# Weights laid out by the host, and no transposes in the fold of the cross-attention weights

## The chip, the cores and the metric

The kernel runs on one core of one Trainium2 chip. The metric is the device time of one execution in microseconds (us). The kernel before was run three times: 2549.39, 2549.66 and 2551.5 us, so its median is 2549.66 us. Lower is better.

## What is computed

The reference is one layer of an encoder in float32, on 2048 tokens of width 1024, with 256 memory tokens:

```
u = rms_norm(h, g_mix_pre);  z = u @ w_in                      # 1024 x 2816
y = concat(swa_with_sinks(z[:, :768]), hgrn2(z[:, 768:])) @ w_out
h = h + rms_norm(y, g_mix_post)
u = rms_norm(h, g_x_pre);  m = rms_norm(mem, g_mem)
y = cross_attention(u, m, wq, wk, wv, wo)                      # 4 heads of 256
h = h + rms_norm(y, g_x_post)
u = rms_norm(h, g_ffn_pre)
y = (silu(u @ w_gate) * (u @ w_up)) @ w_down                   # 1024 x 2816, 2816 x 1024
h = h + rms_norm(y, g_ffn_post)
```

## The kernel before, in words

Every large product is made of three products of rounded parts: an operand is split into a high part (a copy rounded by ScalarE, or by GpSimd in a few places) and a low part (the VectorE difference of the operand and its high part), and TensorE adds high x high, high x low and low x high in PSUM. `split2` (lines 997, 999 and 1000 of the profile) does the split, `mm3` (lines 156 to 158) and `products` (lines 1141 to 1143) the three matmuls. The bulk of the run is `products`, on blocks of 512 columns, most of them combined by a scheme with seven products in place of eight.

The run has these stages. The first half of the tokens goes through w_in in `in_first` and `in_block` (0 to about 260 us), where two column blocks at a time are streamed by `streamed` into tiles named sraw. Then the second half goes through w_in in `in_cols` (one column block of 128 per step, tile raw, matmuls at lines 156 to 158), and beside it run the attention (`swa`) and the recurrence (`hgrn`). Around 600 us begins `fold_cross`: it multiplies the cross-attention weights with the memory, so that the query projection and the keys become one matrix, qk_d, and the values and the output projection another, vo_d. After it (from about 770 us) come the products of w_out, of qk_d and of vo_d, and the two halves of the FFN (w_gate and w_up in 1310 to 2220 us, w_down to the end).

`fold_cross` is where this change acts most. It is a generator of steps:

- eight steps for the keys: `columns` loads 128 columns of wk into a tile raw, splits it (tiles whi and wlo) and multiplies it with the memory (24 matmuls of 256 columns);
- eight steps for the queries: a block of 128 rows of wq is loaded into a tile raw, TensorE transposes it in eight 128x128 pieces into two PSUM banks (`transpose_split`, line 124), ScalarE copies each bank to the high part (line 126), VectorE subtracts (line 127), and 24 matmuls of 256 columns follow; the result goes to SBUF (line 343) and to qk_d;
- eight steps for the values, like those for the keys, and eight blocks of wo (lines 363 to 365).

The loop in `mix` weaves these steps with the recurrence: between two steps of `hgrn`, which handle a block of 128 tokens each, stand two steps of the fold. A recurrence step (names k, qq, v, sg, on, W, kt, vt, atz) loads four tiles of 256 KB from z_d, multiplies (lines 900, 927, 938, 939), transposes (lines 911, 916, 956), and ends at line 957: VectorE multiplies the transposed output, which stands in a PSUM bank psg of which there are two, with sg; the store of sg into y_d follows. There is one tile sg: its next load waits until that store has landed, the next line 957 waits for the load, and the next use of the psg bank waits for line 957. There is one tile v as well, two of k and of qq, three of raw, and three pairs of whi and wlo.

All loads and most stores are issued by one queue, SP's, in the order in which they stand in the program; each waits there for its semaphores and holds up those behind it. The order on every engine comes from the order of the code and from a scheduler that reorders the recorded program by its own estimate of time.

Of the kernel before, what the change touches and what calls it, by code (L numbers as in the profile page):

```python
# [18 lines left out]
P = 128  # L19
# [5 lines left out]
KT = D // P  # L25
NFF = DFF // P
# [10 lines left out]
def f32(ap):  # L37
    return ap.bitcast(F32)
# [10 lines left out]
class Layer:  # L49
# [24 lines left out]
    def load(self, dst, src):  # L74
        self.nc.sync.dma_start(dst, src)  # L75
# [53 lines left out]
    def raw_tile(self):  # L129
        self._n += 1  # L130
        return self.wp.tile([P, D], F32, tag="raw", name=f"raw_{self._n}", bufs=3)
# [11 lines left out]
    def wcols(self, w, c0, engine="P"):  # L143

        raw = self.raw_tile()
        self.load(raw.rearrange("p (k c) -> p k c", k=KT), w[:, c0:c0 + P].rearrange("(k p) c -> p k c", p=P))
        hi, lo = self.split_tiles()
        self.split(raw, hi, lo, engine)
        return (hi.rearrange("p (k c) -> p k c", k=KT), lo.rearrange("p (k c) -> p k c", k=KT))
# [135 lines left out]
    def fold_cross(self):  # L285

        nc, ph = self.nc, self.xp
        gx = ph.tile([P, KT], F32, name="gx")
        self.load(gx, self.I["g_x_pre"].rearrange("r (k p) -> p (r k)", p=P))
        nc.vector.tensor_scalar_mul(gx, gx, float(M) ** -0.5)  # L290
        g = self.gain(self.I["g_mem"])
        mT = [ph.tile([P, KT, M], F32R, name=f"mT{i}") for i in range(2)]
        raw_tile = self.raw_tile
        turn = itertools.count()

        def split_tiles():

            if next(turn) % 3 < 2:
                return self.split_tiles()
            self._n += 1  # L300
            return [ph.tile([P, D], F32R, tag=f"w{x}", name=f"w{x}_{self._n}") for x in ("hi", "lo")]

        def columns(w, c0):
            raw = raw_tile()
            self.load(raw.rearrange("p (k c) -> p k c", k=KT), w[:, c0:c0 + P].rearrange("(k p) c -> p k c", p=P))
            hi, lo = split_tiles()
            self.split(raw, hi, lo, "A")
            return [x.rearrange("p (k c) -> p k c", k=KT) for x in (hi, lo)]

        def projected(w):  # L310
            dst = [ph.tile([P, KT, M], F32R, tag=f"kv{i}", name=f"kv{i}_{self._n}") for i in range(2)]
            for j in range(KT):
                wh, wl = columns(w, j * P)
                ps = self.bank("sh"[j % 2])[:, :M]
                self.mm3(ps, [((wh[:, k, :], wl[:, k, :]), (mT[0][:, k, :], mT[1][:, k, :])) for k in range(KT)])
                nc.scalar.activation(dst[0][:, j, :], ps, AF.Copy)
                nc.vector.tensor_tensor(dst[1][:, j, :], ps, f32(dst[0][:, j, :]), ALU.subtract)
                yield dst

        for t in range(M // P):  # L320
            m = raw_tile()
            self.load(m, self.I["mem"][t * P:(t + 1) * P, :])
            u = self.pre_norm(m, g)
            self.transpose_split(u, lambda q: mT[0][:, 4 * q:4 * q + 4, t * P:(t + 1) * P],
                                 lambda q: mT[1][:, 4 * q:4 * q + 4, t * P:(t + 1) * P])
        for kT in projected(self.I["wk_x"]):
            yield
        for d in range(KT):
            wq = raw_tile()
            self.load(wq, self.I["wq_x"][d * P:(d + 1) * P, :])  # L330
            th, tl = split_tiles()
            th = th.rearrange("p (k c) -> p k c", k=KT)
            tl = tl.rearrange("p (k c) -> p k c", k=KT)
            self.transpose_split(wq, lambda q: th[:, 4 * q:4 * q + 4, :], lambda q: tl[:, 4 * q:4 * q + 4, :])
            o = self.io_tile("x")
            for q in range(2):
                ps = self.bank("sh"[q])
                for r in range(2):
                    h = 2 * q + r
                    self.mm3(ps[:, r * M:(r + 1) * M],  # L340
                             [((th[:, j, :], tl[:, j, :]), (kT[0][:, j, :], kT[1][:, j, :])) for j in (2 * h, 2 * h + 1)])
                sl = slice(q * 512, (q + 1) * 512)
                nc.scalar.activation(o[:, sl], ps, AF.Copy, scale=gx[:, d:d + 1])
            self.store(self.qk_d[d * P:(d + 1) * P, :], o)
            yield
        for vT in projected(self.I["wv_x"]):
            yield
        for h in range(4):
            banks = [[self.bank(k) for k in "sh"] for _ in range(2)]
            for i in range(2):  # L350
                j = 2 * h + i
                raw = raw_tile()
                self.load(raw, self.I["wo_x"][j * P:(j + 1) * P, :])
                if j == 2:
                    self.folded = self.traced(mybir.EngineType.SP)
                wh, wl = split_tiles()
                self.split(raw, wh, wl, "A")
                for mt in range(2):
                    ms = slice(mt * P, (mt + 1) * P)
                    ah, al = vT[0][:, j, ms], vT[1][:, j, ms]  # L360
                    for q in range(2):
                        sl = slice(q * 512, (q + 1) * 512)
                        nc.tensor.matmul(banks[mt][q], ah, wh[:, sl], start=(i == 0), stop=False)
                        nc.tensor.matmul(banks[mt][q], ah, wl[:, sl], start=False, stop=False)
                        nc.tensor.matmul(banks[mt][q], al, wh[:, sl], start=False, stop=(i == 1))
                if i == 0:
                    yield
            for mt in range(2):
                o = self.io_tile("x")
                for q in range(2):  # L370
                    nc.scalar.activation(o[:, q * 512:(q + 1) * 512], banks[mt][q], AF.Copy)
                self.store(self.vo_d[(2 * h + mt) * P:(2 * h + mt + 1) * P, :], o)
            yield
# [92 lines left out]
    def in_first(self):  # L466

        nc, I = self.nc, self.I
# [11 lines left out]
        T, raw = {}, {}  # L480
# [106 lines left out]
        for i in range(4):  # L587
            if i == 2:
                next(phases)
                w = self.traced(PE)  # L590
# [10 lines left out]
        for s in range(2):  # L601
            u.append([])
            for q in range(2):
                self._n += 1
                t = self.big.tile([P, 2, 4, 512], F32R, tag="big", name=f"u1_{q}{s}")
# [4 lines left out]
                u[s] += [(t[:, 0, k, :], t[:, 1, k, :]) for k in range(4)]  # L610

        c0 = self.ORDER[0][0] * P
        stream = self.streamed(
            lambda t, j: self.load(t, I["w_in"][j * 512:(j + 1) * 512, c0:c0 + 2 * P].rearrange("(k p) c -> p k c", p=P)),
            4, "p")
        next(stream)
        S = list(stream)
        z = self.pair_tile()
# [10 lines left out]
    def in_block(self, ca, cb, x, ahead, beside, get, plain, between):  # L629


        nc, w = self.nc, self.I["w_in"]
        z = []

        def load(t, j):
            if between and j:
                between()
            for i, c in enumerate((ca, cb)):
                self.load(t[:, :, i * P:(i + 1) * P], w[j * 512:(j + 1) * 512, c * P:(c + 1) * P]
                          .rearrange("(k p) c -> p k c", p=P))  # L640

        def stream(kind):
            for _ in range(3):
                next(iter(get), None)
            return self.streamed(load, 4, kind)
# [1023 lines left out]
    def hidden_blocks(self, b, f):  # L1669
        nc = self.nc  # L1670
        act = {}

        def stream(w):
            return lambda kind: self.streamed(lambda t, j: self.load(
                t, w[j * 512:(j + 1) * 512, f * P:(f + 2) * P].rearrange("(k p) c -> p k c", p=P)), 4, kind, "A")

        def gate(i, j, a, c):
            if i not in act:
                act[i] = self.row_tile()
            d = act[i][:, j * 512:(j + 1) * 512]  # L1680
            if c is not None:
                nc.vector.tensor_tensor(d, a, c, ALU.add)  # L1682
                a = d
            nc.scalar.activation(d, a, AF.Silu)

        done = []

        def up(i, j, a, c):
            d = act[i][:, j * 512:(j + 1) * 512]
            if c is not None:  # L1690
                nc.vector.tensor_tensor(c, a, c, ALU.add)  # L1691
                a = c
            nc.vector.tensor_tensor(d, a, d, ALU.mult)
            done.append((i, j))
            if (i, 1 - j) in done:
                self.store(self.h_d[f + i, :, b * TB:(b + 1) * TB], act[i])

        def nothing():
            return iter(())

        return [(stream(self.I["w_gate"]), gate, nothing, None), (stream(self.I["w_up"]), up, nothing, None)]

    def down_block(self, c, f0, nk, n):
# [97 lines left out]
```

## Time and profile before

| | |
|---|---|
| median of three runs | 2549.66 us (2549.39 to 2551.5) |
| the profiled execution's own time | 2550.57 us |
| its span, first to last instruction | 2548.9 us |
| mean granted TensorE clock | 0.997 |
| TensorE (PE) busy | 2506.6 us, 98% |
| VectorE (DVE) busy | 1797.3 us, 71% |
| ScalarE (ACT) busy | 1263.0 us, 50% |
| DMA queues of SP and of GpSimd, share of 16 engines | 55.1% and 5.0% |
| w_in loads in whole column blocks (raw) | 20 of 512 KB |
| w_in loads in quarter column blocks (sraw) | 44 of 256 KB, 2 of 512 KB |
| wk, wq, wv loads (raw) | 8 of 512 KB each |
| w_gate and w_up loads (sraw) | 44 of 512 KB each |

PE is the matrix engine's matmuls and PEld its weight loads; "L124" is line 124 of the kernel before. A row of a group gives line, engine, operation, tiles (written<-read), shape and count, then busy us and the mean ns of one, then the engine's idle time before them and what ended it. Matmuls overlap one another, so the duration of one is longer than the time from its start to the start of the next. A row of the timeline gives start and length in us; what stands in brackets is idle time before it and who ended it. In the rows by window, PEclk is the granted clock and the DMA share is that of 16 DMA engines, which can pass 1 for a short stretch.

### The profile page before, as it was taken

What the parts mean: (1) busy time and instruction counts of PE and PEld (TensorE: products, weight loads), DVE (VectorE), ACT (ScalarE), POOL (GpSimd) and SP (SyncE); (2) the same over time, 40 slices, a digit from 0 to 9 for tenths busy, and PEclk for the clock granted to TensorE, in tenths of its full rate; (3) what the DMA queues carried; (4) which work ended last, traced back from release to release, by engine and by line L of the source; (5) the groups of instructions that cost most, each with busy time, mean ns of one, the idle gap of its engine ahead of it and who ended that gap; (6) DMA issues with size and microseconds to landing.
All of it is one profiled execution on the core that took longest, in us unless ns stands there. A gap on an engine that the chain in (4) does not pass through costs nothing.

```text
span 2548.9 us, 34298 instructions
## 1 busy us (share of the span) xinstructions
PE 2506.6 (98%) x12006; PEld 2095.8 (82%) x12006; DVE 1797.3 (71%) x2871; ACT 1263.0 (50%) x2635; POOL 376.4 (15%) x540
## 2 busy tenths in 40 slices
PE   9999999999999999999999999999999999999998
PEld 8878888888997778878878888888888888888886
DVE  8885488986556889987876655576566557574766
ACT  5553467664565566566753333353333335443543
POOL 4231344321401112101200000000000000000022
PEclk9999999999999999999999999999999999999999
DMA  6455644773887896866964522254465434564776
GB/s 201 147 165 178 181 138 157 216 241 96 265 303 273 290 338 192 269 217 212 333 215 138 184 91 83 75 206 140 166 207 195 144 115 164 179 191 106 228 174 154
DMA packets 379437, 482.13 MB, mean 189 GB/s; under 512 B 22016, under 2 KB 274944, under 8 KB 379264
## 3 DMA queue, kind: packets, MB, share of 16 engines
q1 hardware_dynamic: 373216, 457.92, 55.1%
q0 software_dynamic: 6048, 22.02, 5.0%
q8 instruction: 94, 1.54, 0.2%
q14 instruction: 79, 0.65, 0.1%
HBM read 313.14 MB, written 166.72 MB: 188 GB/s over the span
## 4 chain that ended last, share of the span: by engine, by line
PE 81%; DVE 6%; DMA 5%; ACT 3%; issue 2%; POOL 1%; SPq 1%; DVEq 0%; POOLq 0%; ACTq 0%
PE psm L1141 22%; PE psm L1143 22%; PE psm L1142 22%; PE psg L158 2%; PE psg L156 2%; PE psg L157 2%; DVE S L1000 1%; DMA raw<-in_wv_x_dram 1%; DVE T L1000 1%; ACT junk L1516 1%; DMA sraw<-pt_d 0%; PE pss L1402 0%; PE pss L854 0%; SPq L75 0%; PE pst L854 0%
## 5 line engine op out<-in xcount | busy, mean ns | idle before, releaser
L1141 PE MATMUL psm<-T,S 128*128 128x512 f32 x2680 | 1034.8, 391 | 16.0 <-ACT part L1156 7.8
L1142 PE MATMUL psm<-T,S 128*128 128x512 f32 x2680 | 1043.3, 390 | 1.6 <-DVE T L1000 1.6
L1143 PE MATMUL psm<-T,S 128*128 128x512 f32 x2680 | 1030.6, 390 | 3.9 <-DVE S L1000 3.9
L1141 PEld LDWEIGHTS psm<-T,S 128*128 128x128 f32 x2680 | 503.6, 188 | 128.8 <-ACT part L1156 12.6
L1143 PEld LDWEIGHTS psm<-T,S 128*128 128x128 f32 x2680 | 503.8, 188 | 111.0 <-DVE S L1000 6.6
L1142 PEld LDWEIGHTS psm<-T,S 128*128 128x128 f32 x2680 | 503.9, 188 | 107.8 <-DVE T L1000 4.1
L997 ACT ACTIVATE S<-sum 128x512 fp32r<-128x512 f32 (+1 forms) x370 | 223.8, 619 | 370.0 <-PE psm L1143 268.0
L1000 DVE TENSOR_TENSOR S<-sraw,S 128x512 fp32r<-128x512 f32 (+1 forms) x315 | 211.4, 680 | 219.4 <-ACT S L997 216.4
L1156 ACT ACTIVATE part<-psm 128x512 f32<-128x512 f32 x285 | 168.4, 596 | 251.2 <-PE psm L1143 233.8
L1000 DVE TENSOR_TENSOR S<-sum,S 128x512 fp32r<-128x512 f32 (+1 forms) x388 | 257.6, 673 | 41.5 <-ACT S L997 37.7
L997 ACT ACTIVATE S<-sraw 128x512 fp32r<-128x512 f32 (+1 forms) x300 | 184.5, 617 | 107.6 <-PE psm L1143 101.9
L1549 POOL DMA_DIRECT2D y_d<-row x16 | 14.1, 879 | 1076.5 <-DVE row L1731 1025.6
L1000 DVE TENSOR_TENSOR T<-row,T 128x1024 fp32r<-128x1024 f32 (+1 forms) x112 | 130.9, 1184 | 27.7 <-ACT T L997 24.8
L156 PE MATMUL psg<-u,whi 128*128 128x512 f32 x320 | 127.7, 399 | 0.8 <-DVE z L728 0.8
L158 PE MATMUL psg<-u,wlo 128*128 128x512 f32 x320 | 127.6, 399 | 0.0
L157 PE MATMUL psg<-u,whi 128*128 128x512 f32 x320 | 127.0, 397 | 0.0
L1516 ACT ACTIVATE junk<-row 128x512 f32<-128x512 f32 x160 | 99.6, 624 | 45.3 <-DVE row L1538 21.7
L997 ACT ACTIVATE T<-row 128x1024 fp32r<-128x1024 f32 (+1 forms) x112 | 113.3, 1030 | 11.2 <-DMA row<-d_s 4.9
L1682 DVE TENSOR_TENSOR row<-psm,part 128x512 f32<-128x512 f32 x66 | 43.7, 687 | 66.5 <-PE psm L1143 66.5
L1691 DVE TENSOR_TENSOR part<-psm,part 128x512 f32<-128x512 f32 x66 | 43.8, 688 | 60.2 <-PE psm L1143 60.0
L1731 DVE TENSOR_TENSOR row<-psm,part 128x512 f32<-128x512 f32 x72 | 49.1, 688 | 49.5 <-PE psm L1143 49.4
L1000 DVE TENSOR_TENSOR wlo<-raw,whi 128x1024 fp32r<-128x1024 f32 x44 | 54.4, 1237 | 39.6 <-ACT whi L997 28.5
(362 smaller groups left out, 3591.5 us busy)
## 6 DMA issues: line engine op xcount, KB each, us to landing
sraw<-in_w_gate_dram SPq DMA_DIRECT2D x44, 512.0 KB, 3.6
sraw<-in_w_up_dram SPq DMA_DIRECT2D x44, 512.0 KB, 3.7
hid_d<-row SPq DMA_DIRECT2D x44, 512.0 KB, 2.6
sraw<-hid_d SPq DMA_DIRECT2D x32, 512.0 KB, 4.0
sraw<-in_w_in_dram SPq DMA_DIRECT2D x44, 256.0 KB, 3.8
z_d<-pair SPq DMA_DIRECT2D x20, 512.0 KB, 3.3
raw<-in_w_in_dram SPq DMA_DIRECT2D x20, 512.0 KB, 5.0
z_d<-z SPq DMA_DIRECT2D x20, 512.0 KB, 3.9
```

Of the source, the lines that this page charges most:

```text
L156: nc.tensor.matmul(ps, ah, bh, start=(i == 0), stop=False)
L157: nc.tensor.matmul(ps, ah, bl, start=False, stop=False)
L158: nc.tensor.matmul(ps, al, bh, start=False, stop=(i == n - 1))
L997: self.nc.scalar.activation(hi, raw, AF.Copy)
L1000: self.nc.vector.tensor_tensor(lo, raw, f32(hi), ALU.subtract)
L1141: nc.tensor.matmul(ps, s[:, 0, k, :], t[:, 0, k, :], start=st, stop=False, **kw)
L1142: nc.tensor.matmul(ps, s[:, 0, k, :], t[:, 1, k, :], start=False, stop=False, **kw)
L1143: nc.tensor.matmul(ps, s[:, 1, k, :], t[:, 0, k, :], start=False, stop=sp, **kw)
L1156: nc.scalar.activation(t, ps, AF.Copy)
L1516: self.nc.scalar.activation(junk, a, AF.Square, scale=float(D) ** -0.5, accum_out=to)
L1691: nc.vector.tensor_tensor(c, a, c, ALU.add)
L1731: nc.vector.tensor_tensor(d, a, b, ALU.add)
```

## The change

The host lays six weights out in another order. w_in, wk and wv become blocks of 128 columns, [block, row in a group of 128, group, column], so that what one partition of a tile raw takes lies in one run of 4 KB where it was eight runs of 512 B. wq becomes transposed blocks of the same kind: the fold's query steps call `columns` (load and split) in place of a load and `transpose_split`. w_gate and w_up become blocks of 256 columns by 512 rows, one run of 4 KB for a partition of a tile sraw where it was four of 1 KB. The streamed w_in tiles are still filled by two loads of 128 columns each, so that a partition's 2 KB in memory land in four pieces of 512 B in the tile; the last block of `in_first` takes four such loads where it was two of 512 KB.

```diff
     def wcols(self, w, c0, engine="P"):
         raw = self.raw_tile()
-        self.load(raw.rearrange("p (k c) -> p k c", k=KT), w[:, c0:c0 + P].rearrange("(k p) c -> p k c", p=P))
+        self.load(raw, w[c0 // P].rearrange("p k c -> p (k c)"))
...
         def columns(w, c0):
             raw = raw_tile()
-            self.load(raw.rearrange("p (k c) -> p k c", k=KT), w[:, c0:c0 + P].rearrange("(k p) c -> p k c", p=P))
+            self.load(raw, w[c0 // P].rearrange("p k c -> p (k c)"))
             hi, lo = split_tiles()
             self.split(raw, hi, lo, "A")
...
         for d in range(KT):
-            wq = raw_tile()
-            self.load(wq, self.I["wq_x"][d * P:(d + 1) * P, :])
-            th, tl = split_tiles()
-            th = th.rearrange("p (k c) -> p k c", k=KT)
-            tl = tl.rearrange("p (k c) -> p k c", k=KT)
-            self.transpose_split(wq, lambda q: th[:, 4 * q:4 * q + 4, :], lambda q: tl[:, 4 * q:4 * q + 4, :])
+            th, tl = columns(self.I["wq_x"], d * P)
...
-        stream = self.streamed(
-            lambda t, j: self.load(t, I["w_in"][j * 512:(j + 1) * 512, c0:c0 + 2 * P].rearrange("(k p) c -> p k c", p=P)),
-            4, "p")
+        def load(t, j):
+            for i, c in enumerate(self.ORDER[0]):
+                self.load(t[:, :, i * P:(i + 1) * P], I["w_in"][c, :, 4 * j:4 * j + 4, :])
+        stream = self.streamed(load, 4, "p")
...
             for i, c in enumerate((ca, cb)):
-                self.load(t[:, :, i * P:(i + 1) * P], w[j * 512:(j + 1) * 512, c * P:(c + 1) * P]
-                          .rearrange("(k p) c -> p k c", p=P))
+                self.load(t[:, :, i * P:(i + 1) * P], w[c, :, 4 * j:4 * j + 4, :])
...
             return lambda kind: self.streamed(lambda t, j: self.load(
-                t, w[j * 512:(j + 1) * 512, f * P:(f + 2) * P].rearrange("(k p) c -> p k c", p=P)), 4, kind, "A")
+                t, w[f // 2, j]), 4, kind, "A")
...
+    for name in ("w_in", "wk_x", "wv_x"):
+        w = host[name]
+        host[name] = np.ascontiguousarray(w.reshape(KT, P, w.shape[1] // P, P).transpose(2, 1, 0, 3))
+    host["wq_x"] = np.ascontiguousarray(host["wq_x"].reshape(KT, P, KT, P).transpose(0, 3, 2, 1))
+    for name in ("w_gate", "w_up"):
+        host[name] = np.ascontiguousarray(host[name].reshape(2, 4, P, NFF // 2, 2 * P).transpose(3, 0, 2, 1, 4))
```

The order of the instructions changes in the query steps of the fold and hardly anywhere else; lines of the changed kernel are three lower there (line 897 is line 900 before, 924 is 927, 935 and 936 are 938 and 939).

This is TensorE's row before, at the end of one recurrence step and the beginning of the next, with block 13's k and qq and the third query block (raw_999); ident marks a transpose, kv is the memory's keys:

```order
L927 MATMUL psg_993_7394<-vt12_7261,kt12_7254 128x128
L900 MATMUL psg_994_7408<-qq13_7403,k113_7401 128x192 x2
L900 MATMUL pst_995_7413<-qq13_7403,k113_7401 128x192 x2
L124 MATMUL pss_1001_7443<-ident_78,raw_999_7439 128x128 x4
L124 MATMUL psh_1002_7450<-ident_78,raw_999_7439 128x128 x4
L916 MATMUL pst_997_7428<-ident_78,v13_7405 128x128 x4
L156 MATMUL pss_1004_7458<-kv0_900_6649,whi_1000_7441 128x256
L157 MATMUL pss_1004_7458<-kv1_900_6650,whi_1000_7441 128x256
L911 MATMUL psg_996_7421<-ident_78,k113_7401 128x128 x4
L956 MATMUL psg_1013_7535<-ident_78,on12_7383 128x128 x4
```

And this is the same place now; ahead of it stand the transposes of on11 (line 953, into the bank psg_984) and seven of the eight matmuls of lines 935 and 936:

```order
L936 MATMUL pst_985_7351<-W11_7223,q612_7248 128x128
L897 MATMUL pst_991_7391<-qq13_7381,k113_7379 128x192 x2
L924 MATMUL psg_989_7372<-vt12_7263,kt12_7256 128x128 x4
L156 MATMUL pss_998_7424<-kv0_900_6651,whi_996_7419 128x256
L897 MATMUL psg_990_7386<-qq13_7381,k113_7379 128x192 x2
L157 MATMUL pss_998_7424<-kv1_900_6652,whi_996_7419 128x256
L158 MATMUL pss_998_7424<-kv0_900_6651,wlo_996_7420 128x256
```

The transposes of raw are gone, the fold's matmuls stand in longer runs, and between the transposes of on into one psg bank and the second psg bank after it (psg_990, which takes that first bank again) stand fewer instructions: eight matmuls of lines 935 and 936, two of line 897, four of line 924 and one of line 156.

SP's queue before, from the load of sg11 on:

```order
L75 DMA sg11_7199<-z_d_57 128x4x128
L75 DMA qq14_7574<-z_d_57 128x4x128
L75 DMA raw_1006_7487<-in_wq_x_dram 128x1024
L75 DMA v13_7405<-z_d_57 128x4x128
L75 DMA k114_7572<-z_d_57 128x4x128
L78 DMA y_d_58<-sg11_7199 128x512
L75 DMA z_998_7435<-in_w_out_dram 128x2x512
L75 DMA sg12_7371<-z_d_57 128x4x128
```

SP's queue now, from the same load on:

```order
L75 DMA sg11_7201<-z_d_57 128x4x128
L75 DMA qq14_7528<-z_d_57 128x4x128
L75 DMA v13_7383<-z_d_57 128x4x128
L75 DMA k114_7526<-z_d_57 128x4x128
L75 DMA z_994_7413<-in_w_out_dram 128x2x512
L78 DMA qk_d_64<-x_976_7276 128x1024
L75 DMA raw_1038_7714<-in_wq_x_dram 128x1024
L78 DMA y_d_58<-sg11_7201 128x512
L78 DMA qk_d_64<-x_981_7312 128x1024
L75 DMA raw_1043_7750<-in_wq_x_dram 128x1024
L75 DMA qq15_7677<-z_d_57 128x4x128
L75 DMA sg12_7349<-z_d_57 128x4x128
```

The query loads and the qk_d stores have moved ahead in the queue, and between the store of sg11 and the load of sg12 now stand a store, a load of wq and the load of qq15, where it was one load of w_out.

## The prediction

> **What bounds the kernel now.** I read the page first: the busy times, the chain of work that ended last, then busy time by window, then TensorE's waits.
>
> ```profile
> span 2548.9 us, 34298 instructions
> PE 2506.6 (98%) x12006; PEld 2095.8 (82%) x12006; DVE 1797.3 (71%) x2871; ACT 1263.0 (50%) x2635; POOL 376.4 (15%) x540
> PE psm L1141 22%; PE psm L1143 22%; PE psm L1142 22%; PE psg L158 2%; PE psg L156 2%; PE psg L157 2%; DVE S L1000 1%; DMA raw<-in_wv_x_dram 1%; DVE T L1000 1%; ACT junk L1516 1%; DMA sraw<-pt_d 0%; PE pss L1402 0%; PE pss L854 0%; SPq L75 0%; PE pst L854 0%
> ```
>
> TensorE is busy for 2506.6 of 2548.9 us, and two thirds of the chain are its matmuls. Only 42 us are left in which it does nothing, so a faster transfer can give little, and work taken off TensorE gives its whole time wherever nothing else is late. The change has both. I look at the windows of the places that it touches: the fold (600 to 800 us) and the two halves of the FFN's first product.
>
> ```profile
> 600.00:720.00 120.00, 119.58 (x904) 113.90 (x903) 62.19 (x94) 61.51 (x154) 34.14 (x42) 1.00 0.69 208
> 720.00:800.00 80.00, 77.62 (x435) 67.49 (x434) 41.69 (x51) 46.23 (x81) 3.74 (x5) 0.98 0.88 312
> 1310.00:1760.00 450.00, 449.31 (x1985) 371.57 (x1985) 272.01 (x402) 175.61 (x299) 0.00 (x0) 1.00 0.39 130
> 1760.00:2220.00 460.00, 460.00 (x2031) 381.02 (x2030) 286.76 (x440) 176.54 (x317) 0.00 (x0) 1.00 0.48 164
> ```
>
> The columns are the window, then busy us of PE, PEld, DVE, ACT and POOL, the clock, the DMA share and GB/s. In the FFN TensorE is never idle: the 88 loads of w_gate and w_up, changed in shape, are hidden, and I count nothing for them. From 600 to 720 us TensorE loses 0.4 of 120 us while VectorE and ScalarE are half idle: time taken off TensorE there should show in full. From 720 to 800 us it loses 2.4 us.
>
> **The transposes.** Eight query blocks have eight transposes each, 64 in all.
>
> ```profile
> L124 PE MATMUL pss<-ident,raw 128*128 128x128 f32 x32 | 4.8, 272 | 0.0
> L124 PE MATMUL psh<-ident,raw 128*128 128x128 f32 x32 | 4.8, 272 | 0.0
> ...
> 671.87 0.60 PE L124 MATMUL pss<-ident,raw 128*128 128x128 f32 x4
> 672.31 0.60 PE L124 MATMUL psh<-ident,raw 128*128 128x128 f32 x4
> 672.75 0.60 PE L916 MATMUL pst<-ident,v 128*128 128x128 f32 x4
> ```
>
> One lasts 272 ns, but they overlap: four start at 671.87, the next four at 672.31, the next group at 672.75. A group of four takes 0.44 us of TensorE's time, and 16 groups 7.0 us. There is no idle time before them, so they are on TensorE's path: **-7.0 us**. [...]
>
> **What takes their place on ScalarE and VectorE.**
>
> ```profile
> L126 ACT ACTIVATE whi<-pss 128x512 fp32r<-128x512 f32 x8 | 4.8, 594 | 1.3 <-PE pss L124 1.3
> L127 DVE TENSOR_TENSOR wlo<-pss,whi 128x512 fp32r<-128x512 f32 x8 | 5.5, 691 | 3.9 <-ACT whi L126 3.8
> L997 ACT ACTIVATE whi<-raw 128x1024 fp32r<-128x1024 f32 x15 | 15.9, 1060 | 20.4 <-DMA raw<-in_wv_x_dram 9.9 <-PE psg L157 4.2 <-PE pss L157 3.5
> L1000 DVE TENSOR_TENSOR wlo<-raw,whi 128x1024 fp32r<-128x1024 f32 x15 | 18.9, 1259 | 17.4 <-ACT whi L997 17.4
> ```
>
> Lines 126 and 127 have eight such in each of two banks. ScalarE does eight copies of 1.06 us (8.5) where it did 16 of 0.59 (9.5); VectorE eight of 1.26 (10.1) where it did 16 of 0.69 (11.0). Both get a little lighter. A block is ready 2.3 us after its load lands, about as before, and three pairs of whi and wlo let it be split while earlier blocks are multiplied: zero. Without that cover it would cost up to 2.3 us a block.
>
> **The loads.** Alone, a 512 KB load in 512 B runs (wk) and one in 4 KB runs (wq) land almost alike; in traffic the difference is larger.
>
> ```profile
> raw<-in_wk_x_dram SPq DMA_DIRECT2D x1, 512.0 KB, 4.1
> ...
> raw<-in_wq_x_dram SPq DMA_DIRECT2D x1, 512.0 KB, 3.9
> ...
> 722.00:738.00 16.00, 15.83 (x134) 15.63 (x133) 10.51 (x12) 8.72 (x13) 0.76 (x1) 1.00 1.04 320
> 754.00:762.00 8.00, 8.00 (x31) 6.36 (x31) 3.67 (x3) 5.41 (x8) 0.00 (x0) 0.85 1.04 413
> ```
>
> At the same full share the engines moved 320 GB/s where wv's short runs were mixed in and 413 GB/s where the runs were 2 to 4 KB. So 512 KB cost 1.64 us there against 1.27, and with three raw buffers, so up to three loads in a queue, a load lands 0.2 us (alone) to 1.1 us (the last of three) sooner. The 20 loads of w_in blocks and 16 of wk and wv gain it; the streamed w_in loads keep 512 B pieces in the tile and gain from nothing to as much. Two more issues on SP are 0.4 us each of a queue that is not waited for there. None of this is on TensorE's path except in one place, the wait with which the 2.4 us above begin:
>
> ```profile
> 739.66 1.06 ACT L997 ACTIVATE whi<-raw 128x1024 fp32r<-128x1024 f32 x1 [2.41 <-DMA raw<-in_wv_x_dram]
> 748.00 0.63 ACT L997 ACTIVATE S<-sraw 128x512 fp32r<-128x512 f32 x1 [3.31 <-DMA sraw<-y_d]
> 750.74 0.37 ACT L316 ACTIVATE kv<-psh 128x256 fp32r<-128x256 f32 x1
> 752.35 0.51 PE L363 MATMUL psh<-whi,kv 128*128 128x512 f32 x1 [2.21 <-DVE kv L317]
> ...
> 750.00:758.00 8.00, 5.79 (x19) 4.48 (x19) 5.66 (x7) 6.11 (x11) 0.00 (x0) 0.79 1.04 411
> ```
>
> The last wv block is late (ScalarE waits 2.41 us for it), so its buffers come free late, so the loads of wo and y_d behind them start late, ScalarE waits 3.31 us for y_d with the copy of the last values (line 316) queued behind, and TensorE waits 2.21 us. After that the clock is at 0.79 for 8 us, which is 1.7 us more. Earlier wv loads shorten this by 0.2 us to all of it (3.9 us); I take **-1.0 us**, about the last of three, since the DMA share there is full.
>
> **What may come late in its place.** The query steps move the same bytes in less time. The tightest loop there is that of sg.
>
> ```profile
> L957 DVE SCALAR_TENSOR_TENSOR sg<-psg,onorm,sg x7: 743/751/752, 647.7 to 713.1; 128x512 f32<-128x512 f32 x7
> ...
> y_d<-sg SPq DMA_DIRECT2D x7, 256.0 KB, 4.8
> sg<-z_d SPq DMA_DIRECT2D x7, 256.0 KB, 2.8
> ...
> y_d<-sg SPq DMA_DIRECT2D x1, 256.0 KB, 7.2
> ...
> sg<-z_d SPq DMA_DIRECT2D x1, 256.0 KB, 6.0
> ...
> DVE sg L957 <- DMA sg<-z_d: 2.7, 1, 2.7
> ```
>
> The rows are line 957's 0.75 us, the medians of its store and load from 645 to 722 us, and the slowest pair: the store issued at 688.6 took 7.2 us and the load after it 6.0, so that turn of the loop took 14.0 us; a median one takes 0.75 + 4.8 + 2.8 = 8.4 us. VectorE waited for sg only once. How long it may take is read from TensorE's row:
>
> ```profile
> 667.89 0.39 PE L938 MATMUL pst<-vt,atz 128*128 128x128 f32 x2
> ...
> 669.68 1.06 PE L927 MATMUL psg<-vt,kt 128*128 128x128 f32 x8
> 670.57 0.82 PE L900 MATMUL pst<-qq,k 128*128 128x192 f32 x4
> 671.22 0.81 PE L900 MATMUL psg<-qq,k 128*128 128x192 f32 x4
> ...
> 687.19 0.60 PE L956 MATMUL psg<-ident,on 128*128 128x128 f32 x4
> ...
> 696.62 0.81 PE L900 MATMUL psg<-qq,k 128*128 128x192 f32 x4
> ...
> 699.66 0.60 PE L956 MATMUL psg<-ident,on 128*128 128x128 f32 x4
> ```
>
> A recurrence step lasted 12.5 us (687.19 to 699.66) and now loses 16 transposes, 1.76 us: 10.7 us. In the old order the psg bank was asked for again 8.8 us after the transposes of on (687.79 to 696.62). In the new one come before it lines 938 and 939 (667.89 to 669.68, 1.8 us), 927 (0.9), two of 900 (0.65) and one matmul: 3.4 us, of which line 957 needs 0.75. So a turn of up to 10.7 + 2.7 = 13.4 us costs nothing once, and longer ones, or several above 10.7 in a row, make TensorE wait. With a median of 8.4 us I count one late turn: **+0.8 us** (between 0 and 7).
>
> **The sum** is -7.0 - 1.0 + 0.8 = -7.2 us: 2550.57 becomes 2543.4 for the profiled execution, and 2549.66 becomes **2542.5 us** for the median, since that execution is 0.9 us above it.
>
> **Rivals.**
> - *The wait at 752 us goes entirely*, with its low clock, and sg costs nothing: -7.0 - 3.9 gives 2538.8 us. For it: 2.41 us of waiting for the last wv block are as long as TensorE's wait. Against it: ScalarE also waits for y_d, which has no new shape. 0.20.
> - *The sg loop sets the pace*, at about 12.5 us as today: the four recurrence steps beside the queries keep their length, TensorE waits where it transposed, and only the wv gain is left: 2548.7 us. For it: SP's new row puts more between the store and the load of sg, and the DMA share is at 0.69 to 0.88. Against it: the median turn of 8.4 us. 0.20. It is also the case in which the transposes were not really the limit.
> - *Slower: the sg loop at 14 us or more*, as its worst turn was. Then four steps last 14.0 in place of 12.5 us, +6.0, and each wait of over 2 us brings a spell of low clock at 1.7 us (as at 750 us), +6.8, with the wv gain lost as traffic lags: 2562 us. It decides from about 13.9 us in each of the four turns. 0.05. [...]
> - *Other places shift*: in the second half of w_in the loads land a little earlier, and TensorE's many short waits there can fall otherwise. From 260 to 485 us it loses 2.0 us, from 485 to 600 us 3.7:
>
> ```profile
> 260.00:485.00 225.00, 223.02 (x1281) 193.68 (x1280) 176.04 (x434) 137.85 (x413) 85.56 (x129) 0.99 0.54 160
> 485.00:600.00 115.00, 111.34 (x582) 92.43 (x581) 102.65 (x252) 70.09 (x194) 32.32 (x48) 1.00 0.70 214
> ```
>
>   I let half of that, 3 us, go either way, to 2539.5 or 2545.5. 0.10.
>
> **How the numbers follow.** My forecast has 0.45, between 2540.5 and 2545. About 0.2%, 5.1 us, is what a measurement of this kernel can tell from no change: faster is below 2544.6. Of my own case some 0.38 lies below it, with 0.20 of the first rival and half of the last 0.63; slower is the third rival and a little of the last, 0.07; the rest, 0.30, is the same. The range runs from 2538 to 2549.5, which leaves out the slower rival and the tails.
>
> **What would show it.** Right: no line 124 with raw; TensorE still over 99% busy from 600 to the end of the queries, about 7 us shorter; copies of 1.06 us for wq; line 363's wait under 1.5 us; 512 KB loads of w_in, wk and wv in 4 KB packets, packets under 2 KB fewer by about 80,000. Wrong: TensorE waiting at line 897 for VectorE's line 954, or at the wq products for wlo; sg loops over 13.5 us; new spells of low clock between 640 and 800 us. If the fold is 7 us shorter and the total is not, a later wait grew, and the place to look is 800 to 960 us.

## The result and the profile after

The changed kernel takes **2538.27 us** in the median of six runs (2533.83 to 2540.51); the kernel before, run beside it, 2549.52 (six runs, 2546.95 to 2551.5). The ratio is 0.9959, 95% interval 0.9949 to 0.9969: 8 to 13 us less. The profiled execution took 2537.71 us.

First the page of the changed kernel: the span, the busy times, the line on its DMA packets and SP's queue.

```profile
span 2536.0 us, 34175 instructions
PE 2495.5 (98%) x11942; PEld 2085.2 (82%) x11942; DVE 1795.1 (71%) x2863; ACT 1261.0 (50%) x2627; POOL 378.1 (15%) x540
...
DMA packets 314445, 482.13 MB, mean 190 GB/s; under 512 B 22048, under 2 KB 194080, under 8 KB 314272
...
q1 hardware_dynamic: 308224, 457.92, 54.2%
```

The span is 12.9 us shorter. TensorE is busy 11.1 us less and idle 1.8 us less (2548.9 - 2506.6 = 42.3 before, 40.5 now). It runs 64 matmul instructions less. The packets under 2 KB went from 274,944 to 194,080, as forecast, and the same bytes take 54.2% of the DMA engines' time where they took 55.1%: small packets cost little here.

The two windows of the fold, in the same columns as before:

```profile
600.00:720.00 120.00, 119.45 (x897) 113.66 (x896) 65.87 (x94) 66.99 (x161) 36.77 (x44) 1.00 0.74 233
720.00:800.00 80.00, 78.89 (x423) 67.50 (x422) 45.93 (x54) 45.47 (x74) 2.53 (x3) 1.00 0.79 292
```

In the two windows of the FFN nothing changed (TensorE is busy for 449.31 and 460.00 us, as before). From 720 to 800 us TensorE's idle time went from 2.4 to 1.1 us and the clock from 0.98 to 1.00. The wait at 752 us is now this one, in TensorE's row, then ScalarE's and SP's rows ahead of it:

```profile
744.42 0.50 PE L358 MATMUL psh<-whi,kv 128*128 128x512 f32 x1 [0.82 <-DVE kv L317]
```

```profile
740.07 1.16 ACT L994 ACTIVATE S<-sraw 128x512 fp32r<-128x512 f32 x2 [2.29 <-DMA sraw<-y_d]
...
742.59 0.36 ACT L316 ACTIVATE kv<-psh 128x256 fp32r<-128x256 f32 x1
```

```profile
728.39 6.12 SPq L75 DMA_DIRECT2D raw<-in_wo_x_dram  x3
734.60 1.93 SPq L75 DMA_DIRECT2D sraw<-y_d  x4
```

The wait is 0.82 us where it was 2.21, and no low clock follows it. The matmul that waits starts 7.93 us earlier than before (752.35). So 7.9 of the 12.9 us are there by then; the rest comes behind that place, 1.7 of it where low clock used to follow.

### The profile page after: what moved, and what is told of

Same layout as the page of the kernel before. It is cut to its first block, busy times and chain, and to the rows that moved or that the text cites. A ratio compares the mean times of both kernels' runs of the same rounds, so it can differ in the third digit from the quotient of the medians.

```text
span 2536.0 us, 34175 instructions
## 1 busy us (share of the span) xinstructions
PE 2495.5 (98%) x11942; PEld 2085.2 (82%) x11942; DVE 1795.1 (71%) x2863; ACT 1261.0 (50%) x2627; POOL 378.1 (15%) x540
## 2 busy tenths in 40 slices
DMA packets 314445, 482.13 MB, mean 190 GB/s; under 512 B 22048, under 2 KB 194080, under 8 KB 314272
## 3 DMA queue, kind: packets, MB, share of 16 engines
q1 hardware_dynamic: 308224, 457.92, 54.2%
## 4 chain that ended last, share of the span: by engine, by line
PE 78%; DVE 8%; DMA 7%; issue 3%; ACT 3%; POOL 1%; SPq 1%; DVEq 0%; POOLq 0%; ACTq 0%
PE psm L1140 21%; PE psm L1138 21%; PE psm L1139 21%; PE psg L158 2%; PE psg L157 2%; PE psg L156 2%; DVE T L997 1%; DVE S L997 1%; DMA qd<-z_d 1%; DVE sum L1113 1%; DVE row L1407 1%; DMA h1t_d<-row 0%; DMA y_d<-sg 0%; DMA qk_s<-extra 0%; ACT junk L1513 0%
## 5 line engine op out<-in xcount | busy, mean ns | idle before, releaser
L1138 PEld LDWEIGHTS psm<-T,S 128*128 128x128 f32 x2680 | 502.9, 188 | 126.9 <-ACT part L1153 12.9
L994 ACT ACTIVATE T<-row 128x1024 fp32r<-128x1024 f32 (+1 forms) x112 | 113.4, 1032 | 11.1 <-DMA row<-in_w_down_dram 3.8
L997 DVE TENSOR_TENSOR wlo<-raw,whi 128x1024 fp32r<-128x1024 f32 x52 | 64.1, 1233 | 34.3 <-ACT whi L994 22.7
```

The lines of the kernel that those rows point to most:

```text
L994: self.nc.scalar.activation(hi, raw, AF.Copy)
L997: self.nc.vector.tensor_tensor(lo, raw, f32(hi), ALU.subtract)
L1138: nc.tensor.matmul(ps, s[:, 0, k, :], t[:, 0, k, :], start=st, stop=False, **kw)
```

## Where 12.9 us come from

The granted clock in TensorE's records of the kernel before falls to half for 3.41 us at 278 and at 753 us and for 6.83 us at 821 us. These are windows of the kernel before, each pair the stretch ahead of such a one and the stretch itself (columns as above, the clock third from the right):

```profile
749.61:753.02 3.41, 1.20 (x6) 0.66 (x5) 3.23 (x6) 3.25 (x7) 0.00 (x0) 1.00 1.05 416
753.02:756.43 3.41, 3.41 (x10) 2.64 (x9) 1.41 (x2) 2.78 (x5) 0.00 (x0) 0.50 1.04 402
...
817.87:821.28 3.41, 1.41 (x5) 0.51 (x4) 1.56 (x4) 2.70 (x7) 1.97 (x4) 1.00 1.06 376
821.28:828.11 6.83, 6.23 (x15) 4.88 (x16) 6.83 (x9) 1.68 (x5) 2.44 (x3) 0.50 1.04 349
```

TensorE was idle for 2.2 of 3.41 us (1.20 busy), and in the next 3.41 us it ran at half clock, which costs up to 1.7 us, half of that time. Before the last microseconds the kernel before has four such stretches, the 6.83 us counted as two (the one at 278 us the changed kernel also has), the changed one has one. Three stretches fewer are at most 5.1 us. In the pair of profiles the 12.9 us can therefore be put down to 7.0 for 64 transposes, 4.1 for the clock (not measured by itself: what is left of the 11.1 us of busy time), and 1.8 of idle time.

The stretch at 821 us followed two waits, of 1.72 and 0.88 us, that end at 820.26 and 821.88 us. The first and the third profile of the changed kernel have two waits of the same lengths there, ending at 811.32 and 812.94 and at 807.79 and 809.40 us, with no low clock behind them (1.00 from 790 to 960 us); its second has low clock from 809.18 us on, behind 1.72 us of idle time. Over all runs the mean granted clock is 0.9978 for the changed kernel (16 runs) and 0.9975 for the one before (the 84 runs beside the experiments): 0.0003 of 2549 us is 0.8 us in the mean, where the pair of profiles has 4. So most of that part belongs to these two executions. Two more measurements of the changed kernel below gave ratios of 0.9963 and 0.9967, so 9.4 and 8.4 us less. The mean of the three, **9.4 us**, is what has to be explained.

## The experiments

Three theories stood at first. A: TensorE's time and the new order of instructions make the gain. B: the transposes make 7 us and the layouts, with fewer small packets, the rest. C: what is over 7 us is low clock that falls at random.

**wq alone, and the layouts alone.** The first kernel is the one before with only wq's blocks (a load and a split for wq, no line 124); the second is the changed one with wq as before:

```diff
 (1) the kernel before, with
-            self.load(wq, self.I["wq_x"][d * P:(d + 1) * P, :])
+            self.load(wq, self.I["wq_x"][d].rearrange("p k c -> p (k c)"))
...
-            self.transpose_split(wq, ...)
+            self.split(wq, th, tl, "A")
...
 (2) the changed kernel, with
-            th, tl = columns(self.I["wq_x"], d * P)
+            wq = raw_tile()
...
+            self.transpose_split(wq, ...)
```

> wq alone is laid out transposed; w_in, wk, wv, w_gate and w_up keep the old layout, and TensorE's row of instructions is that of the changed kernel. Theory A (the order and TensorE's time make the whole gain: 7.0 us of transposes, and up to 4 us of waits and low clock between 740 and 830 us, which the new order shortens): about 2538.5 us, within 2 us of the changed kernel. Theory B (the transposes are 7.0 us, the other 4.2 us of the gain come from the layouts, which leave fewer small packets): about 2542.5 us. Theory C (what is over 7 us is a difference of low clock that falls at random): 2538 to 2543, with low clock spells at 753 or 821 us in some profiles and not in others.

> All the new layouts but wq's, which is transposed on TensorE as before; TensorE's row of instructions is that of the kernel before. Theory A: no change, 2549.5 us within 1.5. Theory B: faster by about 4.2 us, 2545.3. Theory C: 2549.5, or up to 4 us less where the low clock at 753 and 821 us is absent from the profile.

**The transposes put back.** In the changed kernel, four transposes of the identity go into each query bank ahead of its products. Nothing is left out; nobody reads them.

```diff
                 ps = self.bank("sh"[q])
+                for j in range(4):
+                    nc.tensor.transpose(ps[:, j * P:(j + 1) * P], self.ident, self.ident)
```

> The changed kernel with 64 transposes of the identity put back where the old ones stood (eight per query block, into the bank that the query's products then overwrite; nobody reads them, so no result depends on them). ScalarE, VectorE and the loads stay as changed. Theory A, in its strict form (TensorE's time is the price): slower than the changed kernel by 7.0 us, 2545.3; if the new order of waits is part of it, up to 2 us more as the old pacing comes back. Rival (the price was in the copies out of PSUM, or in the wait for them): 0 to 2 us slower, since 64 transposes would then fit into idle time.

**The changed kernel again, twice.**

> The changed kernel again, unchanged. Theory C: if the low clock at 753 and 821 us is a matter of the single run, a second profile has one or both of them, with the same waits ahead; span up to 3.7 us longer. Theory A in its strict form: no low clock there again, since the wait at 752 us is below what brings it.

> The changed kernel once more, unchanged, beside the two others. Low clock at random: a third profile with 1 to 4 spells of 3.41 us, in places that the first two did not have or had not all of; each spell follows a stretch of 3.41 us in which TensorE was idle for over about 1.5 us. Time 10 to 11 us under before.

**The layouts by parts, and wk and wv put back.** The first two are the kernel before with w_gate and w_up alone, and with w_in, wk and wv alone, in the new layout. The third is the changed kernel, where `strided` is `columns` with the old load of eight runs of 512 B:

```diff
-                wh, wl = columns(w, j * P)
+                wh, wl = strided(w, j * P)
...
-    for name in ("w_in", "wk_x", "wv_x"):
+    for name in ("w_in",):
```

> The kernel before with w_gate and w_up alone in the new layout; instructions of TensorE, VectorE and ScalarE in the order of before. Prediction's count: no change, 2549.3 us within 1.5. Rival (the layouts' 1.9 us come from the FFN): 2547.4.

> The kernel before with w_in, wk and wv alone in the new layout; wq, w_gate and w_up as before; instructions of TensorE, VectorE and ScalarE in the order of before. If the 1.9 us of the layouts are here (shorter waits at 260 to 600 us, where w_in's second half streams, or at 750 us): 2547.4 us. If the layouts change nothing and 1.9 us was spread of the runs: 2549.3 within 1.5.

> The changed kernel with wk and wv back in the old layout (8 runs of 512 B for a partition); the instructions of all engines stand in the same order. If the blocks of wv in one run are what shortened TensorE's wait near 743 us (0.99 us in the changed kernel, under 0.4 in its two other profiles): the wait is back at 2 to 3 us, as it is with the new order and all old layouts (2.97), the last wv loads land 0.5 us or more later, and the kernel is 1.5 to 4 us slower than the changed one, 2540 to 2542 where before is 2549. If the order alone shortened it: the wait stays under 1 us and the time within 1 us of the changed kernel.

What they gave (the ratio is to the kernel before in the same batch, whose medians were 2547.2 to 2549.9; the last columns are TensorE's idle time and the clock from 740 to 790 us, the end of the fold):

| kernel | median us | ratio, 95% interval | idle us | clock |
|---|---|---|---|---|
| before | 2549.52 | | 2.21 | 0.97 |
| layouts alone | 2547.59 | 0.9991 (0.9982 to 0.9999) | 2.73 | 0.97 |
| w_gate, w_up alone | 2549.90 | 1.0006 (0.9998 to 1.0015) | 2.35 | 0.97 |
| w_in, wk, wv alone | 2548.34 | 1.0001 (0.9992 to 1.0010) | 2.96 | 0.97 |
| wq alone | 2539.57 | 0.9966 (0.9955 to 0.9978) | 2.80 | 0.97 |
| changed, wk and wv old | 2541.97 | 0.9975 (0.9964 to 0.9986) | 1.98 | 0.97 |
| changed, 64 transposes back | 2545.21 | 0.9989 (0.9980 to 0.9997) | 1.84 | 1.00 |
| changed | 2538.27 | 0.9959 (0.9949 to 0.9969) | 1.12 | 1.00 |
| changed, second time | 2539.96 | 0.9963 (0.9950 to 0.9976) | 0.59 | 1.00 |
| changed, third time | 2538.51 | 0.9967 (0.9955 to 0.9980) | 0.37 | 1.00 |

*The transposes are about 7 us.* Put back, they cost 0.0026 of 2549 us, 6.6, against the changed kernel of the same batch, and not the 0 to 2 us of the rival; the two intervals together leave 2.6 to 10.6. The scheduler also placed some other instructions of TensorE's row differently there, and the wait for the values is 1.84 us, so not all of the 6.6 need be the transposes' own time. In that kernel's trace they are groups of 32 in each of the two banks again, with no idle time before them:

```profile
L334 PE MATMUL pss<-ident 128*128 128x128 f32 x32 | 4.8, 273 | 0.0
```

*Theory A has the time of wq alone right, 2539.57 us, but not its reason:* the wait in the fold is there in full, 2.80 us idle, with the new order. By its ratio this kernel is 8.6 us faster than the one before (5.6 to 11.5), 0.8 us less than the changed kernel's mean.

*Theory B falls as it was put.* The two halves of the layouts change nothing that can be measured. Together they came out 2.3 us faster with an interval that just leaves out zero; the parts do not bear that out, and the wait in the fold is as long as before, so I count at most some 2 us, not shown.

*In the traces, wk and wv in one run shorten the wait once the order is new.* With the old layout of wk and wv every engine's instructions stand in the same order as in the changed kernel, and the wait is back, with its low clock. These are TensorE's rows of that kernel (lines 904, 365 and 961 there are 897, 358 and 954 of the changed one), and the wait of the kernel with wq alone:

```profile
704.27 0.92 PE L904 MATMUL psg<-qq,k 128*128 128x192 f32 x4 [1.15 <-DVE sg L961]
...
744.19 0.79 PE L365 MATMUL psh<-whi,kv 128*128 128x512 f32 x1 [1.98 <-DVE kv L324]
```

```profile
743.77 0.79 PE L362 MATMUL psh<-whi,kv 128*128 128x512 f32 x1 [2.80 <-DVE kv L317]
```

The wait is 1.98 and 2.80 us where the three profiles of the changed kernel have 0.82 and twice none worth a row. The first matmul after it lasts 0.79 us, where it is 0.50 us in the changed kernel. The four loads of wv issued from 708 to 728 us landed in a median of 5.4 us with wk and wv old and 4.8 in the changed kernel, but in 5.4 and 5.3 in its two other profiles, so that median does not tell the layouts apart. The seventh of the eight wv loads does, and with it the load of w_out issued just ahead, whose shape did not change (wk and wv old, then changed):

```profile
z<-in_w_out_dram SPq DMA_DIRECT2D x1, 512.0 KB, 6.5
raw<-in_wv_x_dram SPq DMA_DIRECT2D x1, 512.0 KB, 6.4
```

```profile
z<-in_w_out_dram SPq DMA_DIRECT2D x1, 512.0 KB, 5.1
raw<-in_wv_x_dram SPq DMA_DIRECT2D x1, 512.0 KB, 4.9
```

With wq alone both took 6.1 us; in the two other profiles of the changed kernel w_out's took 5.6 and wv's 5.4 and 5.3. So in the traces neither the order nor the layout shortens the wait alone; both together do. What that is worth in the runs is less sure. With wk and wv old the ratio is 0.9975 against a mean of 0.9963 for the changed kernel, 3 us, and the intervals leave 0 to 6; wq alone, with the longer wait, is only 0.8 us above that mean. Neither difference is clear of noise.

*Theory C holds for the pair of profiles.* Of the two places in question the second profile of the changed kernel has low clock at one, from 809.18 us on, where the first has none; the third has it at neither (1.00 from 600 to 740, 740 to 790 and 790 to 960 us).

**How the wait hangs together.** In SP's row the loads of y_d stand right behind the third wo load, and that load waits for a raw buffer, held until VectorE has split the last wv blocks (SP's rows of the kernel before, then of wq alone):

```profile
736.06 6.28 SPq L75 DMA_DIRECT2D raw<-in_wo_x_dram  x3
742.39 2.18 SPq L75 DMA_DIRECT2D sraw<-y_d  x4
```

```profile
727.98 6.14 SPq L75 DMA_DIRECT2D raw<-in_wo_x_dram  x3
734.22 2.39 SPq L75 DMA_DIRECT2D sraw<-y_d  x4
```

From the issue of y_d to the matmul that waits pass 9.96 us before (742.39 to 752.35), 9.55 with wq alone, 9.65 with wk and wv old and 9.82 in the changed kernel: landing, ScalarE's copies of y_d, the copy of the last values behind them in its row. These four are nearly the same. What differs is the lead, from the issue of y_d to the moment TensorE runs dry: 7.75, 6.75, 7.67 and 9.00 us. The wait is what the lead lacks.

The way from issue to matmul is not fixed, though. It is 9.97 us with w_gate and w_up alone and 10.20 with the layouts alone, but 11.00 with w_in, wk and wv alone and 11.91 with 64 transposes back, where the first load of y_d took 6.6 and 7.5 us to land (5.1 to 5.8 in the six others). So the last of these has the longest lead, 10.07 us, and still waits 1.84.

The lead begins when VectorE has split the wv block whose buffer the third wo load takes. In the three profiles of the changed kernel this split ends 2.2, 2.9 and 2.9 us before TensorE begins the last wv block; with wk and wv old it is 0.9 us, with wq alone none. That fits wv blocks that land sooner. Two pairs of edits tested the two links of this chain.

**The copies of the values on VectorE** (in the changed kernel, and in the one before), so that they do not stand behind y_d on ScalarE:

```diff
-                nc.scalar.activation(dst[0][:, j, :], ps, AF.Copy)
+                copy(dst[0][:, j, :], ps)
...
-        for vT in projected(self.I["wv_x"]):
+        for vT in projected(self.I["wv_x"], nc.vector.tensor_copy):
```

> The changed kernel with the eight copies of the value projection (line 316 with wv) on VectorE instead of ScalarE, where the last of them stands behind a copy that waits for y_d. Theory Y (TensorE's wait at 743 us is ScalarE's wait for y_d, passed on by its queue): that wait is gone or under 0.4 us, with the low clock behind it, and the kernel is 0.5 to 1.5 us faster than the changed one in the median. Theory W (the wait comes from the late wv loads, as the prediction put it): the wait stays at 0.8 us or more when a wv load is late, and the time is that of the changed kernel within 0.5 us.

> The kernel before with the same edit: wv's copies on VectorE; transposes and layouts as before. Theory Y: the 2.4 us wait at 750 us and the low clock behind it (1.7 us in the runs that have it) go, while ScalarE still waits over 3 us for y_d: 2.4 to 4.1 us faster, about 2546 us. Theory W: the wait moves to the products of the last wv block or stays, less than 1 us faster.

Measured: 2540.71 us, 0.9976 (0.9967 to 0.9984), and 2551.18 us, 1.0014 (1.0005 to 1.0022): both slower than without the edit, by 3 us against the changed kernel (the mean of its ratios) and by 3.6 against the one before. TensorE's row of the first:

```profile
739.98 0.50 PE L359 MATMUL psh<-whi,kv 128*128 128x512 f32 x1 [0.31 <-DVE kv L318]
743.42 0.50 PE L359 MATMUL pss<-whi,kv 128*128 128x512 f32 x1 [1.77 <-ACT x L367]
756.10 0.51 PE L359 MATMUL pss<-whi,kv 128*128 128x512 f32 x1 [0.78 <-ACT whi L995]
757.36 0.51 PE L360 MATMUL pss<-wlo,kv 128*128 128x512 f32 x1 [0.53 <-DVE wlo L998]
```

Theory Y was half right. The wait for the values is 0.31 us, but ScalarE still waits for y_d (4.03 us), and now the copies of wo's products (line 367) stand behind it: a bank is not freed, and TensorE waits 1.77 us for that. In the other kernel the wait for the values is 0.40 us, with no low clock behind it, and TensorE waits 0.76 us for the low part of a wv block, 1.00 for a copy of wo's products and 0.77 for parts of wo. So the idle time from 740 to 790 us is 3.14 us in the first kernel and 3.05 in the second, where it was 2.21. That accounts for 0.8 of the 3.6 us; the rest is open.

**y_d one load earlier in SP's queue:**

```diff
-                if j == 2:
+                if j == 1:
                     self.folded = self.traced(mybir.EngineType.SP)
```

> The changed kernel with the four loads of y_d one load earlier in SP's queue: ahead of the third wo load, which waits for a raw buffer, instead of behind it. Theory Q (the wait near 743 us is the queue: y_d's loads stand behind a load that waits for a buffer): ScalarE's wait for y_d goes from 2.3 us to under 0.5, and TensorE's wait with it; the time is that of the changed kernel or up to 1 us less, 2537.5 to 2539.5 where before is 2549. Rival (the third wo load, now behind 1 MB of y_d, is late in its place): a wait of 1 to 3 us for whi at the wo products, and no gain or up to 2 us slower.

> The kernel before with the same edit alone. Theory Q: the 2.4 us wait at 750 us goes, and the low clock that followed it: 2.4 to 4.1 us faster than before. Rival: a wait for wo takes its place, within 1 us of before or slower.

In the kernel before: 2545.70 us, 0.9993 (0.9985 to 1.0002), a gain of 1.8 us that does not leave zero out, where Q said 2.4 to 4.1. Its rows show why:

```profile
747.08 0.50 PE L363 MATMUL pss<-whi,kv 128*128 128x512 f32 x1 [0.74 <-ACT whi L997]
748.34 0.50 PE L364 MATMUL pss<-wlo,kv 128*128 128x512 f32 x1 [0.53 <-DVE wlo L1000]
763.90 0.49 PE L363 MATMUL pss<-whi,kv 128*128 128x512 f32 x1 [0.32 <-ACT x L371]
```

The one wait of 2.21 us became three that make 1.59, and no low clock followed (1.00). TensorE's wait for the values is gone, as Q said, and waits for wo stand in its place, as the rival said, though shorter than its 1 to 3 us. Q's other sign did not come: ScalarE still waits for y_d, 3.00 us here (3.31 before) and 3.22 in the changed kernel (2.29 without the edit), where the first of these loads took 7.2 and 7.0 us to land and not 5.5 and 5.4:

```profile
734.21 1.15 ACT L994 ACTIVATE S<-sraw 128x512 fp32r<-128x512 f32 x2 [3.22 <-DMA sraw<-y_d]
```

That wait merely stands further ahead of TensorE: the copies of the last two value blocks come behind it, and no matmul waits for them.

In the changed kernel: **2533.30 us** (2532.83 to 2535.61 in five runs), 0.9949 (0.9935 to 0.9963), beside 2538.51 (2536.34 to 2540.58) of the changed kernel in the same batch. It beats both kernels, by more than expected and not for the reason tried: the end of the fold could give 0.4 us at most (the idle time there in the changed kernel's third profile), and from 600 to 790 us TensorE is in fact idle for 0.74 us with the edit and 0.37 without. These are TensorE's waits from 800 to 1060 us in the changed kernel's third profile, then in this one (total us, times, longest):

```profile
PE psm L1138 <- ACT S L994: 2.7, 2, 1.7
PE psm L1140 <- DVE S L997: 1.5, 3, 0.7
PE psm L1138 <- ACT T L994: 1.4, 1, 1.4
PE psm L1138 <- DVE row L1591: 1.3, 1, 1.3
PE psm L1138 <- ACT part L1153: 1.2, 2, 0.9
```

```profile
PE psm L1140 <- DVE S L997: 1.9, 3, 0.9
PE psm L1138 <- ACT S L994: 1.7, 1, 1.7
PE psm L1138 <- ACT part L1153: 1.2, 2, 0.9
PE psm L1138 <- ACT T L994: 0.8, 1, 0.8
```

8.1 us became 5.6: of line 994's two waits one is gone, and that for line 1591. Over the whole span the idle time went from 41.2 to 36.8 us, so these rows are a little over half of it. With y_d earlier the scheduler also put some of ScalarE's copies S ahead of others in the stage after the fold. Whether that is the cause was not tried apart; in the kernel before, the same edit gave 1.8 us, within noise.

## Why the prediction was right where it was, and where not

The forecast was 2542.5 us in a range of 2538.0 to 2549.5. The measured 2538.27 lies 0.27 us inside the range's lower end, and where the rival with the wait gone stood, 2538.8, to which the prediction gave 0.20; the two later medians, 2539.96 and 2538.51, also lie below the 2540.5 to 2545 of its own case. That the first one fell inside the range was partly luck. The direction, the place and the largest term were right.

- **Transposes, -7.0:** right. Put back, they cost 6.6 (2.6 to 10.6). TensorE's share of the chain was read too low there: the two thirds are the lines of `products` alone, and the page gives 81% for the whole engine, which only strengthens the argument.
- **Copies at nothing:** right. In the fold from 600 to 722 us ScalarE's and VectorE's rows of the split, wq's among them, cost what line 997's and 1000's cost before, and ScalarE waits for TensorE there, not TensorE for it:

```profile
L994 ACT ACTIVATE whi<-raw 128x1024 fp32r<-128x1024 f32 x20 | 21.2, 1059 | 14.3 <-PE psh L157 5.1 <-PE pss L157 5.0 <-PE psg L157 4.2
```

```profile
L997 DVE TENSOR_TENSOR wlo<-raw,whi 128x1024 fp32r<-128x1024 f32 x20 | 25.0, 1250 | 11.6 <-ACT whi L994 11.6
```

- **w_in, w_gate and w_up at nothing:** right within the 2 us that the runs can tell (1.0006 and 1.0001). The gain of 0.2 to 1.1 us a load came for wk alone. From issue to landing, the medians of the fourteen profiles are 4.5 to 4.6 us for wk in the old layout and 4.0 to 4.2 in the new; for w_in's whole blocks they are 5.0 to 5.2 and 4.8 to 5.3, for all eight wv loads 6.1 to 7.0 and 5.6 to 7.2, for w_gate and w_up 3.6 to 3.9 and 3.7 to 4.0.
- **wv and the wait at 752 us, -1.0:** the weakest step. By the traces the place and the direction were right and the size was not: 1.4 us of the wait went in the profiled execution and nearly all of 2.2 in the two others, with the low clock behind it in all three, so 3 to 4 us. The load's gain of 0.2 to 1.1 us was put in the wait's place one to one; but the wait is what the lead of y_d's issue lacks, and with the new layout and the new order together that lead was 1.25 us longer. In the runs the term is not clear of noise: the two kernels with the new order and the longer wait are 0.8 and 3 us slower than the changed one. The argument against the rival (ScalarE also waits for y_d, which has no new shape) was wrong: the first y_d load lands as slowly as before (5.4 us, before 5.5), but it is issued further ahead of TensorE, since it stands behind wo in SP's queue.
- **One late turn of sg, +0.8:** it came once, and smaller:

```profile
705.67 0.92 PE L897 MATMUL psg<-qq,k 128*128 128x192 f32 x4 [0.25 <-DVE sg L954]
```

  Behind the old layout of wk and wv it is 1.15 us, in the two other profiles of the changed kernel there is none. So by the traces -7.0, -3 to -4 and 0 to 0.5 make about 10 us, where the three measurements have a mean of 9.4. But wq alone, without the second term, has 8.6 already, so either that term is smaller in the runs or the new order brings 1 to 2 us of its own; intervals of 3 us each way cannot tell.
- **A recurrence step of 10.7 us:** a little more; the transposes of on start 11.0 us apart, where one step before took 12.5:

```profile
679.39 0.60 PE L953 MATMUL psg<-ident,on 128*128 128x128 f32 x4
690.40 0.60 PE L953 MATMUL psg<-ident,on 128*128 128x128 f32 x4
```

- **The slower rival** did not come: no wait of over 2 us, and no low clock from 600 to 800 us. Its spell of low clock for each wait of over 2 us was the author's estimate from the one wait of 2.21 us at 752 us.
- **Low clock behind the fold** was in no term. In the pair of profiles it is two stretches, over 3 us; in the mean of the runs it is small.

## What to carry to other kernels

Where TensorE is the bound, price operations taken off its row by their distance from start to start (0.44 us for four here, 7.0 in the sum, 6.6 when put back), and not by their duration. Wider packets gave nothing measurable here where no load was waited for (a ratio of 1.0006 with w_gate and w_up alone). For a wait on a late transfer follow the chain back to the instruction that issues it, and ask how far ahead of the waiting engine that issue is, and how long the way from issue to use is: the wait is what the lead lacks (2.21 us here before, 9.96 less 7.75), and both can move. An edit that moves one load can also change the order that the scheduler makes elsewhere (4.9 us between two means here, for a cause that is open), so read the waits behind it too.

## What was not expected of the hardware

In the trace of the kernel before the half clock begins at 278.56, 753.02 and 821.28 us; these starts are 474.46 and 68.26 us apart, 139 and 20 times 3.413 us. In the 3.41 us ahead of the stretches looked at here TensorE was idle for between 0.95 and 2.32 us. The most, 2.32 us, is that with wq alone, where the wait of 2.80 us falls (the interval with the wait, then the next):

```profile
739.88:743.29 3.41, 1.09 (x5) 0.56 (x3) 3.03 (x4) 3.16 (x7) 0.00 (x0) 1.00 1.02 372
743.29:746.71 3.42, 2.94 (x7) 2.36 (x8) 1.63 (x4) 2.57 (x5) 0.00 (x0) 0.50 1.04 413
```

In the kernel before, 2.21, 2.00 and 1.18 us of idle time stand in the 3.41 us ahead of 753.02, 821.28 and 278.56 us; in the changed kernel only 0.95 us stand ahead of the stretch at 278.85 us. Longer idle times than these last two came without it: 1.50 us from 500.43 us on in the kernel before and 1.49 us from 500.72 us on in the changed one, with a clock of 1.00 in the next interval of both. So the "over about 1.5 us" that was expected for the third profile does not hold for the stretch at 278 us in either trace. With 1.72 it followed in one profile (the changed kernel's second) and not in another (its first):

```profile
805.77:809.18 3.41, 1.69 (x6) 1.13 (x7) 0.70 (x1) 2.88 (x7) 1.70 (x5) 1.00 1.07 365
809.18:812.59 3.41, 3.41 (x9) 2.63 (x9) 3.41 (x6) 0.00 (x0) 0.00 (x0) 0.50 0.98 231
```

```profile
807.91:811.32 3.41, 1.69 (x8) 1.07 (x6) 2.34 (x4) 2.60 (x8) 1.99 (x4) 1.00 1.04 388
811.32:814.73 3.41, 2.53 (x10) 1.79 (x11) 2.49 (x4) 2.06 (x5) 2.08 (x3) 1.00 1.10 369
```

So in these traces idle time alone does not tell when half clock comes, and what does stays open. The mean clocks of the runs differ by 0.8 us only, so whether the change itself makes the stretch behind the waits near 810 us rarer or this is chance stays open too.
